# A decoder trunk on one core: the opening loop rebuilt (c broadcast through the identity, squares in three partial sums, no GpSimd products, a fixed order per k-tile, a seventh output tile)

## The chip, the core and the metric

The kernel runs on one core of one Trainium2 chip. The metric is the device time of one execution in microseconds (us); lower is better. The engines are TensorE (PE; its weight loads are PEld), VectorE (DVE), ScalarE (ACT), GpSimd (POOL) and SyncE (SP, which here only issues transfers). All numbers are float32. A product that has to keep float32 accuracy is made of "float32r" matmuls: each operand is split into a high part (h) and a remainder (l), and three matmuls h·h, l·h and h·l are added up in PSUM.

## The reference, cut to what matters

The sequence has 1024 tokens of width 1024, one layer. Around the change the reference computes this:

```python
c_act = jax.nn.silu(c)                          # c: (1, 1024)
mod = c_act @ ada_w[l] + ada_b[l]               # 6 x 1024 values
sh1, sc1, g1, sh2, sc2, g2 = jnp.split(mod, 6, axis=-1)
h = modulate(rmsnorm(x), sh1, sc1)              # h*(1+sc1)+sh1
u, q, k, v, r, z = jnp.split(h @ w_in[l], IN_SPLITS, axis=-1)
y_pool = pool_mixer(u, ...)                     # windows of 2, 4, 8, 16
y_gla = gla_mixer(q, k, v, r, z, ...)           # chunked gated linear attention
y = jnp.concatenate([y_pool, y_gla], axis=-1) @ w_out[l]
x = x + g1[:, None, :] * y
h = modulate(rmsnorm(x), sh2, sc2)
x = x + g2[:, None, :] * conv_ffn(h, ...)       # up, conv of width 3, silu, down
return rmsnorm(x) * final_norm
```

## The kernel before, in words

Everything is kept transposed: 128 channels on the partitions, tokens along the free dimension. The tokens are worked on as two halves of 512 (`hf` 0 and 1), the 1024 channels as eight k-tiles (`NK`). A matmul of 128x128 weights with 512 tokens is the unit of PE's work.

**The opening.** Eight tiles `x0[k]` of the first half are loaded. Line 230 (`sumsq_step`) squares each on ACT and line 234 adds the squares on DVE into one tile `nsa`; a float32 matmul with a matrix of ones (line 243, `ss`) sums over the partitions and spreads the sum, and ACT makes 1/rms of it with Ln and Exp (lines 245 and 246, `nr`). Meanwhile two float32 matmuls of `ones[0:1]` with the row `crow` spread c over all partitions, and ACT takes the silu of the PSUM tiles (line 558, `cb`). Six matmuls `warm` with no use stand at three places (`keep_warm`).

**The opening loop** goes over the eight k-tiles. For tile k it needs one column of sh1 and one of sc1. `mod_tile(t)` (line 214) makes one such column: it loads 128 rows of ada_w transposed (`ada`, 512 KB), multiplies with `cb` and sums along the row; a last small DVE instruction (line 225) adds the bias into `modv`. In its fast form product and sum are one DVE instruction (line 219). In its slow form POOL makes the product (line 222) and ACT the sum (line 223). The loop makes the shift columns k = 1 to 7 the slow way, and the shift of k = 0 and all scale columns the fast way. Then, for the tile: `mod_head` (line 267, DVE, `x`), the split of the weights `wh` (line 152, ACT) and `wl` (line 153, DVE), and `mod_split`: `hh` (line 274, ACT) and `hl` (line 275, DVE). PE then makes 3 matmuls for each of six output tiles (q, k, two of r) and 2 for the gate input z (`pz`), so 20 per k-tile. All seven results accumulate in PSUM over the eight k-tiles.

**After the loop** a list of jobs, each one output tile of a projection (24 matmuls of 512 tokens), fills PE: first r2 and r3 of the first half, then v, the four u, then the second half (`k0 z q0 k1 v0..v3 q1`, `r0..r3`, `u0..u3`), the output projection, and the MLP. Beside them runs the gated linear attention (GLA): two gate matmuls `gp`, then for each half and each of two channel tiles seven levels of scores `sc`, state products `sp`, outputs `op` and norms `on`. These are spawned as "sides" that come due at times of the planner's own clock, which adds up the matmuls' sizes; PE's order is written out by hand in this way (`manual_schedule` for PE), while the other engines' order is made by a scheduler. A job can hold PE's order back until a side has got to a point (`until`): job q0 and q1 of the second half do so until the first half's GLA outputs stand in the order.

Of the kernel before, what the change touches and what calls it, by code (L numbers as in the profile page):

```python
# [53 lines left out]
def trunk_kernel(ctx, tc, xT, cvec, adaT, vecs, w_start, w_z, w_qkru, w_v, w_g2, w_pool,  # L54
# [94 lines left out]
    def split_w(raw, shape=(P, NK, P)):  # L149
        wh = wp.tile(list(shape), F32R, tag="wh", name="wh")  # L150
        wl = wp.tile(list(shape), F32R, tag="wl", name="wl")
        act.copy(out=wh, in_=raw)  # L152
        dve.tensor_tensor(out=wl, in0=raw, in1=wh.bitcast(F32), op=ALU.subtract)  # L153
# [33 lines left out]
    crow = raw4("crow", (1, NK * P))  # L187
    nc.scalar.dma_start(out=crow, in_=cvec)
# [25 lines left out]
    def mod_tile(t, fast, where=None):  # L214
        a = raw4(name="ada", shape=(P, NK * P)) if where is None else tmp(where, shape=(P, NK * P))
        nc.sync.dma_start(out=a, in_=adaT[t])
        acc = const.tile([P, 1], F32, name="macc", tag="macc", bufs=4)
        if fast:
            dve.scalar_tensor_tensor(out=a, in0=a, scalar=1.0, in1=cb, op0=ALU.mult,  # L219
                                     op1=ALU.mult, accum_out=acc)  # L220
        else:
            pool_e.tensor_tensor(out=a, in0=a, in1=cb, op=ALU.mult)
            act.activation(out=a, in_=a, func=AF.Copy, accum_out=acc)
        one_plus = 8 <= t < 16 or 32 <= t < 40
        dve.scalar_tensor_tensor(out=modv[:, t:t + 1], in0=acc, scalar=1.0 if one_plus else 0.0,
# [11 lines left out]
    def rstd_of(acc, own=None):  # L237
# [7 lines left out]
        act.activation(out=r, in_=out, func=AF.Ln, bias=epsb, scale=1.0 / 1024)
        act.activation(out=r, in_=r, func=AF.Exp, scale=-0.5)
# [19 lines left out]
    def mod_head(x, t, r, sc_c, k):  # L266
        dve.scalar_tensor_tensor(out=t, in0=x, scalar=modv[:, sc_c + k:sc_c + k + 1], in1=r,
                                 op0=ALU.mult, op1=ALU.mult)
        return t

    def mod_split(t, sh_c, k):
        h, l = s2(F32R, name="hh"), s2(F32R, name="hl")
# [1 line left out]
        act.activation(out=h, in_=t, func=AF.Identity, bias=sh, scale=1.0)  # L274
        mark["split"] = dve.scalar_tensor_tensor(out=l, in0=t, scalar=sh, in1=h.bitcast(F32),  # L275
                                                 op0=ALU.add, op1=ALU.subtract)
# [276 lines left out]

    keep_warm(6)
    for n in range(2):
        cps = ptile()
        mm(cps, ones[0:1], crow[:, n * T:n * T + T], True, True)
        last = act.activation(out=cb[:, n * T:n * T + T], in_=cps, func=AF.Silu)
# [742 lines left out]
```

## Time and profile before

| what | value |
|---|---|
| median of 3 runs | 1050.42 us (1049.86 to 1051.85) |
| the profiled execution | 1047.94 us |
| its span, first to last instruction | 1046.2 us |
| mean granted PE clock | 0.989 |
| PE busy in the span | 1001.2 us (96%) |
| DVE busy | 854.6 us (82%) |
| ACT busy | 549.2 us (52%) |
| POOL busy | 190.5 us (18%) |

The profiled execution is 2.5 us shorter than the median of the runs, and 1.7 us longer than its span. PE's records are pipelined: matmuls of 512 tokens that follow each other start about 0.23 us apart, though each record is about 0.39 us long, so the distance between starts is what counts. A row of the timeline gives start, length, engine, line, operation, output<-input, shapes, count, and in brackets the idle time of the engine before it with what ended it. Several executions of a row can stand together with their count.

### The profile page before, as it was taken

To read this page: it belongs to the slowest core of one execution; us is meant where nothing else is said; L and a number is where in the kernel's file an instruction comes from. 1 tells how busy PE (TensorE), PEld (TensorE's weight loads), DVE (VectorE), ACT (ScalarE), POOL (GpSimd) and SP (SyncE) were. 2 spreads that over 40 slices of the span, in tenths; PEclk is the share of its full clock that TensorE was granted. 3 is DMA by queue.
4 is the path that set the end of the run, shared out by engine and by line. 5 is a ranking of instruction groups with operands and counts; after the bars stand their busy time and mean duration, and the time that the engine had idled before them with its cause. 6 is when DMAs were issued, how large, how long until landed. Compare 5 with 4: busy or idle time off the path is not lost.

```text
span 1046.2 us, 12684 instructions
## 1 busy us (share of the span) xinstructions
PE 1001.2 (96%) x4481; PEld 815.4 (78%) x4481; DVE 854.6 (82%) x1197; ACT 549.2 (52%) x888; POOL 190.5 (18%) x163
## 2 busy tenths in 40 slices
PE   7989999998999989999999999999999999999995
PEld 5768868886777768877888888888888788888874
DVE  7967899689988849999977788777776776988883
ACT  5465585442733547665555455555554544644442
POOL 3437203222141030011100101101001000200210
PEclk8999999999999999999999999999999999999998
DMA  8743232455487442233222222332334787223642
GB/s 315 258 151 111 81 110 83 149 174 182 149 280 262 155 167 81 86 137 129 105 99 91 105 102 107 131 111 101 111 111 151 272 283 240 101 81 111 201 141 81
DMA packets 60817, 154.21 MB, mean 147 GB/s; under 512 B 6641, under 2 KB 9809, under 8 KB 60754
## 3 DMA queue, kind: packets, MB, share of 16 engines
q1 hardware_dynamic: 54192, 134.00, 37.8%
q0 software_dynamic: 4928, 17.30, 4.3%
q10 hardware_dynamic: 1634, 2.10, 0.6%
q8 instruction: 35, 0.57, 0.2%
q14 instruction: 28, 0.23, 0.1%
HBM read 127.69 MB, written 25.69 MB: 147 GB/s over the span
## 4 chain that ended last, share of the span: by engine, by line
PE 62%; DVE 23%; DMA 5%; ACT 4%; issue 4%; POOL 2%; SPq 0%; POOLq 0%; ACTq 0%; DVEq 0%
PE dn L107 18%; PE upy L107 14%; PE upx L107 9%; PE upz L107 9%; PE pp L107 8%; DVE wl L153 3%; DVE ada L219 2%; DMA ada<-in_adaT_dram 2%; DVE xs L802 2%; DVE hl L275 2%; POOL le L347 1%; DVE la L376 1%; DVE ua L812 1%; DVE lq L359 1%; PE ss L107 1%
## 5 line engine op out<-in xcount | busy, mean ns | idle before, releaser
L107 PE MATMUL dn<-xs 128*128 128x512 f32 (+1 forms) x480 | 111.1, 386 | 1.7 <-DVE xs L802 1.3
L107 PE MATMUL dn<-ws 128*128 128x512 f32 x456 | 108.3, 394 | 2.3 <-DVE xs L1110 2.3
L107 PEld LDWEIGHTS dn<-xs 128*128 128x128 f32 x480 | 88.5, 188 | 21.1 <-DVE xs L802 2.1
L107 PEld LDWEIGHTS dn<-ws 128*128 128x128 f32 x456 | 86.7, 190 | 20.9 <-issue 2.7
L107 PE MATMUL upy<-sh,xs 128*128 128x512 f32 x264 | 86.6, 390 | 2.1 <-DVE cb L944 2.1
L107 PE MATMUL upy<-sh,ws 128*128 128x512 f32 x264 | 86.4, 389 | 0.0
L153 DVE TENSOR_TENSOR wl<-raw,wh 128x1024 fp32r<-128x1024 f32 (+1 forms) x50 | 64.2, 1285 | 27.1 <-ACT wh L152 26.8
L997 POOL DMA_DIRECT2D gd<-y x22 | 12.0, 546 | 375.7 <-DVE y L996 358.7
L107 PE MATMUL pp<-hh,wh 128*128 128x512 f32 x176 | 73.7, 419 | 2.7 <-ACT hh L274 1.4
L107 PE MATMUL pp<-hl,wh 128*128 128x512 f32 x176 | 70.8, 402 | 4.8 <-DVE hl L275 4.8
L107 PE MATMUL pp<-hh,wl 128*128 128x512 f32 x176 | 70.8, 402 | 2.6 <-DVE wl L153 2.6
L802 DVE TENSOR_TENSOR xs<-ua,xs 128x512 fp32r<-128x512 f32 x78 | 60.6, 782 | 14.8 <-ACT xs L801 14.8
L802 DVE TENSOR_TENSOR ws<-ua,ws 128x512 fp32r<-128x512 f32 x76 | 55.1, 727 | 15.7 <-ACT ws L801 15.7
L107 PE MATMUL upx<-hh,xs 128*128 128x512 f32 x192 | 62.8, 392 | 2.5 <-DVE x L693 2.5
L801 ACT CAST ws<-ua 128x512 fp32r<-128x512 f32 x76 | 47.0, 622 | 34.4 <-PE upy L107 17.2
L152 ACT CAST wh<-raw 128x1024 fp32r<-128x1024 f32 (+1 forms) x50 | 50.4, 1008 | 26.8 <-DMA raw<-in_w_out_dram 10.8
L801 ACT CAST xs<-ua 128x512 fp32r<-128x512 f32 x78 | 48.1, 622 | 30.5 <-PE upy L107 17.4
L812 DVE TENSOR_TENSOR ua<-ua 128x512 f32<-128x512 f32 x88 | 60.2, 687 | 2.1 <-DMA ua<-in_w_up_dram 0.3
L347 POOL TENSOR_TENSOR le<-b 128x512 f32<-128x512 f32 x24 | 37.1, 1549 | 134.1 <-DVE lq L359 53.8
L107 PE MATMUL upz<-sh,ws 128*128 128x512 f32 x184 | 60.4, 389 | 0.0
L937 DVE SCALAR_TENSOR_TENSOR y<-ca,vec,y 128x1023 f32<-128x1023 f32 (+1 forms) x44 | 56.3, 1280 | 4.3 <-ACT y L934 3.5
L107 PEld LDWEIGHTS upy<-sh,xs 128*128 128x128 f32 x264 | 49.5, 188 | 13.2 <-DVE cb L944 2.9
(261 smaller groups left out, 2521.2 us busy)
## 6 DMA issues: line engine op xcount, KB each, us to landing
ua<-in_w_up_dram SPq DMA_DIRECT2D x49, 512.0 KB, 3.4
ada<-in_adaT_dram SPq DMA_DIRECT2D x32, 512.0 KB, 3.4
gd<-y POOLq DMA_DIRECT2D x22, 512.0 KB, 2.9
raw<-in_w_qkru_dram SPq DMA_DIRECT2D x18, 512.0 KB, 3.3
da<-gd SPq DMA_DIRECT2D x36, 256.0 KB, 2.8
da<-in_w_down_dram SPq DMA_DIRECT2D x36, 256.0 KB, 3.4
raw<-in_w_out_dram SPq DMA_DIRECT2D x16, 512.0 KB, 4.4
x<-in_xT_dram SPq DMA_DIRECT2D x24, 256.0 KB, 4.3
```

What stands on the lines that cost most here:

```text
L107: pe.matmul(out=out, lhsT=lhsT, rhs=rhs, start=start, stop=stop, skip_group_check=more)
L152: act.copy(out=wh, in_=raw)
L153: dve.tensor_tensor(out=wl, in0=raw, in1=wh.bitcast(F32), op=ALU.subtract)
L219: dve.scalar_tensor_tensor(out=a, in0=a, scalar=1.0, in1=cb, op0=ALU.mult, op1=ALU.mult, accum_out=acc)
L275: mark["split"] = dve.scalar_tensor_tensor(out=l, in0=t, scalar=sh, in1=h.bitcast(F32), op0=ALU.add, op1=ALU.subtract)
L347: pool_e.tensor_tensor(out=e.rearrange("p (n h) -> p n h", n=nb), in0=b.rearrange("p (n h) -> p n h", n=nb), in1=bb[:, :, 0, h - 1:h].broa ...
L359: dve.tensor_tensor(out=ql.rearrange("p e (n h) -> p e n h", h=h), in0=q2.rearrange("p e (n two h) -> p e n two h", two=2, h=h)[:, :, :, 1 ...
L801: act.copy(out=h, in_=src)
L802: dve.tensor_tensor(out=l, in0=src, in1=h.bitcast(F32), op=ALU.subtract)
L812: eng.tensor_tensor(out=out, in0=a, in1=b, op=ALU.subtract)
L937: dve.scalar_tensor_tensor(out=y[:, sh:], in0=c[:, :S - sh], scalar=cw[j], in1=y[:, sh:], op0=ALU.mult, op1=ALU.add)
L997: nc.gpsimd.dma_start(out=gd[i], in_=ya)
```

## The change

The opening and its loop are written anew; the work after the loop keeps its code, but for the job r2, which the loop now does itself.

- c comes in as a 128x8 tile `cc`. Its silu is taken once on that small tile. Eight float32 matmuls, with one column of `cc` broadcast as the 128x128 stationary operand and the identity (`ident`, a part of `cft`) as the moving one, make the spread c; ACT copies the two PSUM tiles into `cb` after its last square.
- `cft` is loaded at the start, on ACT's queue, and no longer in the loop.
- The squares of x0..x3 are made on DVE, those of x4..x7 on ACT; they are added in three groups (4, 2, 2), and three matmuls `ss` add the groups in PSUM. The useless matmuls now number 8, 2 and 13.
- Both columns of each k-tile are made the fast way on DVE; the POOL products and the ACT sums of the loop are gone.
- The loads of tile k+2 are issued at tile k (`start_loads`), the ada tiles from five buffers in turn (`lo`, `lr`, `la`, `lb`, `lb`).
- `issue_after` fixes the order of a k-tile: on DVE two products, `mod_head`, `wl`, `hl`; on ACT `hh` of a tile, then `wh` of the next.
- Weights of a seventh output tile, r2, are in `w_start` (448 KB a tile in place of 384), and the loop makes it: 23 matmuls per k-tile in place of 20. Its PSUM tile is the single one of pool `m`. Job r2 is gone from the list after the loop, as `put_r(pq[6], 0, 2)` shows.

```diff
@@ split_w, mod_tile, rstd_of, mod_split
+    def later(inst):
+        return nullcontext() if inst is None else tc.issue_after(inst.ins)
-    def split_w(raw, shape=(P, NK, P)):
+    def split_w(raw, shape=(P, NK, P), act_after=None, dve_after=None):
...
-        act.copy(out=wh, in_=raw)
-        dve.tensor_tensor(out=wl, in0=raw, in1=wh.bitcast(F32), op=ALU.subtract)
+        with later(act_after):
+            act.copy(out=wh, in_=raw)
+        with later(dve_after):
+            mark["wl"] = dve.tensor_tensor(out=wl, in0=raw, in1=wh.bitcast(F32), op=ALU.subtract)
...
-        if fast:
+        with later(late):
             dve.scalar_tensor_tensor(out=a, in0=a, scalar=1.0, in1=cb, op0=ALU.mult,
                                      op1=ALU.mult, accum_out=acc)
-        else:
-            pool_e.tensor_tensor(out=a, in0=a, in1=cb, op=ALU.mult)
-            act.activation(out=a, in_=a, func=AF.Copy, accum_out=acc)
@@ opening
-    keep_warm(6)
-    for n in range(2):
-        cps = ptile()
-        mm(cps, ones[0:1], crow[:, n * T:n * T + T], True, True)
-        last = act.activation(out=cb[:, n * T:n * T + T], in_=cps, func=AF.Silu)
-    exp_ln(last)
-    keep_warm(6)
-    r0 = rstd_of(acc0)
-    keep_warm(6)
-    pq = [ptile() for _ in range(4)]
-    pq += [stile("pr"), stile("pr"), stile("pz")]
+    WARM = (8, 2, 0, 13)
+    def start_loads(k):
+        got = []
+        for t in (k, 8 + k):
+            a = tmp(("lo", "lr", "la", "lb", "lb")[ada_n[0] % 5], shape=(P, NK * P))
+            ada_n[0] += 1
+            nc.sync.dma_start(out=a, in_=adaT[t])
+            got.append(a)
+        raw = raw4(shape=(P, 7, P))
+        nc.sync.dma_start(out=raw, in_=w_start[k])
...
+    last = act.activation(out=cc, in_=cc, func=AF.Silu)
+    exp_ln(last)
+    loads = [start_loads(k) for k in range(2)]
...
+    for k in range(NK):
+        mm(cps[k // 4][:, k % 4 * P:k % 4 * P + P], cc[:, k:k + 1].broadcast_to([P, P]), ident,
+           True, True)
+    keep_warm(WARM[1])
+    ss = stile("ss")
+    parts = []
+    for k in range(NK):
+        sq = s2(name="sq")
+        if k < 4:
+            dve.tensor_tensor(out=sq, in0=x0[k], in1=x0[k], op=ALU.mult)
+        else:
+            last = act.activation(out=sq, in_=x0[k], func=AF.Square)
+        if k in (0, 4, 6):
+            parts.append(sq)
+        else:
+            added = dve.tensor_tensor(out=parts[-1], in0=parts[-1], in1=sq, op=ALU.add)
+        if k in (3, 5, 7):
+            mm(ss, ones, parts[-1], k == 3, k == 7)
...
+    with tc.issue_after(last.ins):
+        for n in range(2):
+            act.copy(out=cb[:, n * T:n * T + T], in_=cps[n])
+    r0 = rstd_from(ss)
+    keep_warm(WARM[3])
+    pq = [ptile() for _ in range(4)]
+    pq += [stile("pr"), stile("pr"), mtile("pr"), stile("pz")]
@@ the loop over k
-        mod_tile(k, k == 0, ("lo", "lr", "la")[k % 3])
-        with tc.issue_after(mark["split"].ins) if k else nullcontext():
-            mod_tile(8 + k, True, "lb")
-        wh, wl = load_w(w_start[k], (P, 6, P))
...
-        hs[0][k] = mod_split(mod_head(x0[k], x0[k], r0, 8, k), 0, k)
+        if k + 2 < NK:
+            loads.append(start_loads(k + 2))
+        after = mark["split"] if k else added
+        for t in (0, 1):
+            after = mod_tile(8 * t + k, loads[k][0][t], after)
+        with tc.issue_after(after.ins):
+            t = mod_head(x0[k], x0[k], r0, 8, k)
+        wh, wl = split_w(loads[k][1], (P, 7, P), mark["hh" if k else "exp"], mark["head"])
+        hs[0][k] = mod_split(t, 0, k, mark["wl"])
...
-        for n in range(6):
+        for n in range(7):
             mm3(pq[n], wh[:, n], wl[:, n], *hs[0][k], k == 0, k == NK - 1)
...
+    put_r(pq[6], 0, 2)
...
-    run_jobs([job_r(0, 2), job_r(0, 3)])
+    run_jobs([job_r(0, 3)])
...
-    a["w_start"] = np.concatenate([q, k, r[:, 0:2 * P]], axis=1).reshape(NK, P, 6, P)
+    a["w_start"] = np.concatenate([q, k, r[:, 0:3 * P]], axis=1).reshape(NK, P, 7, P)
```

Three places show how the instructions move. The first is DVE's order for the second k-tile of the loop, k = 1. Before (`lb` is the ada tile of the scale column, `macc` the sum that goes into `modv`; two sums arrive, one of them from ACT):

```order
L219 SCALAR_TENSOR_TENSOR lb_279,macc_281<-lb_279,cb_154 128x1024
L225 SCALAR_TENSOR_TENSOR modv_153<-macc_275,vec_136 128x1
L225 SCALAR_TENSOR_TENSOR modv_153<-macc_281,vec_136 128x1
L267 SCALAR_TENSOR_TENSOR x_121<-x_121,modv_153,nr_211 128x512
L153 TENSOR_TENSOR wl_287<-raw_284,wh_286 128x768
L275 SCALAR_TENSOR_TENSOR hl_292<-x_121,modv_153,hh_291 128x512
```

And the same tile of the change, where `la` holds the ada tile of the shift column:

```order
L226 SCALAR_TENSOR_TENSOR la_175,macc_306<-la_175,cb_155 128x1024
L232 SCALAR_TENSOR_TENSOR modv_154<-macc_306,vec_138 128x1
L226 SCALAR_TENSOR_TENSOR lb_177,macc_309<-lb_177,cb_155 128x1024
L232 SCALAR_TENSOR_TENSOR modv_154<-macc_309,vec_138 128x1
L277 SCALAR_TENSOR_TENSOR x_123<-x_123,modv_154,nr_229 128x512
L158 TENSOR_TENSOR wl_314<-raw_179,wh_313 128x896
L287 SCALAR_TENSOR_TENSOR hl_318<-x_123,modv_154,hh_317 128x512
```

DVE has one product of 1024 columns more in the tile, and `wl` grew from 768 to 896 columns. The second place is the opening of PE's order, of the change:

```order
L107 MATMUL pp<-ones 128x128 x8
L107 MATMUL pp<-cft,cc 128x128 x8
L107 MATMUL pp<-ones 128x128 x2
L107 MATMUL ss<-sq,ones 128x512 x3
L107 MATMUL pp<-ones 128x128 x13
```

Before it had `warm` x6, two 128x512 matmuls of `crow`, `warm` x6, one `ss` and `warm` x6. The third place is the end of the first half's GLA on PE, channel tile 1. Before, 18 matmuls of job v of the second half (`pp`) stand between the two groups of outputs `op`, and 6 more between the second group and the norm `on`; their first rows are

```order
L107 MATMUL op_1764<-lb_585,st1_156 128x256
L107 MATMUL op_1764<-la_1386,v_1010 128x128 x2
L107 MATMUL pp_1626<-wh_1719,hh_1241 128x512
L107 MATMUL pp_1626<-wh_1719,hl_1242 128x512
L107 MATMUL pp_1626<-wl_1720,hh_1241 128x512
```

and in the change the same place reads, up to the first matmuls of job q1,

```order
L107 MATMUL op_1791<-lb_615,st1_157 128x256
L107 MATMUL op_1791<-la_1420,v_987 128x128 x2
L107 MATMUL op_1807<-lb_615,st1_157 128x256
L107 MATMUL op_1807<-la_1420,v_989 128x128 x2
L107 MATMUL op_1807<-la_1420,v_991 128x128 x2
L107 MATMUL on_1816<-lr_1790,ones_148 128x512
L107 MATMUL on_1820<-lr_1790,ones_148 128x512
L107 MATMUL pp_1849<-hh_1110,wh_1746 128x512
```

The 24 matmuls that stood there have moved ahead, since every job comes one job earlier against the GLA: the two groups of outputs and the two norms now follow each other with nothing between.

More of the change, by code (lines that the diff above doesn't have):

```diff
@@ L186, in trunk_kernel @@
     act.preload_act_table_set("silu_and_others")
-    crow = raw4("crow", (1, NK * P))
-    nc.scalar.dma_start(out=crow, in_=cvec)
+    cc = const.tile([P, NK], F32, name="cc")
+    nc.scalar.dma_start(out=cc, in_=ccol)
+    cft = ga.tile([P, NC_F], F32, name="cft")
+    nc.scalar.dma_start(out=cft, in_=cf)
     x0 = [s2(name="x") for _ in range(NK)]
@@ L212, in trunk_kernel, with mod_tile, mod_store @@
     cb = ga.tile([P, NK * P], F32, name="cb")
[L214 to L217, printed above, removed]
-        if fast:
+    def mod_tile(t, a=None, late=None):
+        if a is None:
+            a = raw4(name="ada", shape=(P, NK * P))
+            nc.sync.dma_start(out=a, in_=adaT[t])
+        acc = const.tile([P, 1], F32, name="macc", tag="macc", bufs=3)
+        with later(late):
             dve.scalar_tensor_tensor(out=a, in0=a, scalar=1.0, in1=cb, op0=ALU.mult,
                                      op1=ALU.mult, accum_out=acc)
-        else:
-            pool_e.tensor_tensor(out=a, in0=a, in1=cb, op=ALU.mult)
-            act.activation(out=a, in_=a, func=AF.Copy, accum_out=acc)
+        return mod_store(t, acc)
+    def mod_store(t, acc):
         one_plus = 8 <= t < 16 or 32 <= t < 40
-        dve.scalar_tensor_tensor(out=modv[:, t:t + 1], in0=acc, scalar=1.0 if one_plus else 0.0,
+        return dve.scalar_tensor_tensor(out=modv[:, t:t + 1], in0=acc, scalar=1.0 if one_plus else 0.0,
                                  in1=vec[:, V_ADAB + t:V_ADAB + t + 1], op0=ALU.add, op1=ALU.add)
@@ L578, in trunk_kernel, with keep_warm @@
                               op=ALU.subtract)
-        hs[0][k] = mod_split(mod_head(x0[k], x0[k], r0, 8, k), 0, k)
+        return got, raw
+    ada_n = [0]
+    last = act.activation(out=cc, in_=cc, func=AF.Silu)
+    exp_ln(last)
+    loads = [start_loads(k) for k in range(2)]
+    idle = ptile()
+    def keep_warm(n):
+        for _ in range(n):
+            mm(idle[:, 0:P], ones, ones, True, True)
+    keep_warm(WARM[0])
+    cps = [ptile() for _ in range(2)]
+    for k in range(NK):
+        mm(cps[k // 4][:, k % 4 * P:k % 4 * P + P], cc[:, k:k + 1].broadcast_to([P, P]), ident,
+           True, True)
@@ new lines, in trunk_kernel @@
+    with tc.issue_after(last.ins):
[5 more added lines that the diff above has]
+    pq += [stile("pr"), stile("pr"), mtile("pr"), stile("pz")]
+    for k in range(NK):
+        if k + 2 < NK:
[7 more added lines that the diff above has]
+        hs[0][k] = mod_split(t, 0, k, mark["wl"])
```

53 lines of the change are left out of this document (26 added, 27 removed).

## The prediction

> **What bounds the kernel now.** I read first the page, then the timeline of each engine over the opening, then the busy time by stretch and the chain of waits behind it.
>
> ```profile
> core 0: us, PE busy (x) PEld busy (x) DVE busy (x) ACT busy (x) POOL busy (x), PEclk, DMA share, GB/s
> 20.00:40.00 20.00, 18.39 (x67) 14.08 (x68) 19.86 (x28) 7.81 (x12) 8.63 (x4) 0.83 0.68 241
> 40.00:60.00 20.00, 18.40 (x80) 13.87 (x79) 18.90 (x27) 10.55 (x17) 8.17 (x6) 1.00 0.61 210
> 130.00:140.00 10.00, 7.89 (x33) 5.66 (x32) 10.00 (x18) 7.19 (x12) 0.02 (x1) 1.00 0.46 157
> ```
>
> PE is the bound of the whole (96% busy in the table above), but not of the opening loop: from 20 to 40 us DVE works 19.86 of 20 us, and PE runs at a mean clock of 0.83. Why DVE is full, the timeline shows:
>
> ```profile
> 14.18 2.36 POOL L222 TENSOR_TENSOR lr<-lr,cb 128x1024 f32<-128x1024 f32 x1 [12.01 <-ACT nr L246]
> 14.21 2.87 DVE L267 SCALAR_TENSOR_TENSOR x<-x,modv,nr 128x512 f32<-128x512 f32 x1 [0.94 <-ACT nr L246]
> 17.87 2.83 DVE L275 SCALAR_TENSOR_TENSOR hl<-x,modv,hh 128x512 fp32r<-128x512 f32 x1
> 25.06 0.95 DVE L153 TENSOR_TENSOR wl<-raw,wh 128x768 fp32r<-128x768 f32 x1
> 25.94 0.75 DVE L275 SCALAR_TENSOR_TENSOR hl<-x,modv,hh 128x512 fp32r<-128x512 f32 x1
> 26.61 1.22 DVE L219 SCALAR_TENSOR_TENSOR lb<-lb,cb 128x1024 f32<-128x1024 f32 x1
> 28.06 0.75 DVE L267 SCALAR_TENSOR_TENSOR x<-x,modv,nr 128x512 f32<-128x512 f32 x1
> 28.73 3.16 DVE L153 TENSOR_TENSOR wl<-raw,wh 128x768 fp32r<-128x768 f32 x1
> ```
>
> The same `x` takes 2.87 us beside a POOL product and 0.75 us without one, `hl` 2.83 against 0.75, `wl` 3.16 against 0.95. So every POOL product costs DVE about 2.1 us. PE shows what comes of it:
>
> ```profile
> 20.76 0.79 PE L107 MATMUL pp<-hl,wh 128*128 128x512 f32 x1 [2.37 <-DVE hl L275]
> 26.90 0.40 PE L107 MATMUL pr<-hh,wh 128*128 128x512 f32 x1
> 38.41 0.50 PE L107 MATMUL pp<-hl,wh 128*128 128x512 f32 x1 [0.85 <-DVE hl L275]
> 48.70 0.39 PE L107 MATMUL pp<-hh,wh 128*128 128x512 f32 x1
> 53.25 0.39 PE L107 MATMUL pp<-hh,wh 128*128 128x512 f32 x1
> 54.27 0.50 PE L107 MATMUL pp<-hl,wh 128*128 128x512 f32 x1 [0.64 <-DVE hl L275]
> 63.30 0.39 PE L107 MATMUL pp<-hh,wh 128*128 128x512 f32 x1
> ```
>
> PE works without a stop only from 20.76 us. A k-tile of 20 matmuls at full clock takes 48.70 to 53.25, so 4.55 us, 0.2275 us a matmul. The 14 matmuls from 20.76 to 26.90 take 6.14 us where 3.19 would do: 2.95 us lost to the half clock. Two waits for `hl` are shown (0.85 and 0.64 us idle, about 1 us each with the start-up); there is a third like them. At 63.30 the loop is over and the first job begins.
>
> **The opening, costed.** When is 1/rms ready, and when the first `hl`?
>
> ```profile
> L191 SPq DMA_DIRECT2D x<-in_xT_dram x8: 397/431/433, 0.8 to 4.0; - x8
> DMA to landing us min/median/max: 2.7/3.7/4.6
> 6.39 0.58 ACT L558 ACTIVATE cb<-pp 128x512 f32<-128x512 f32 x1
> 1.06 2.93 PE L107 MATMUL warm<-ones 128*128 128x128 f32 x12 [1.06 <-DVE oneb L210]
> 10.75 2.04 PE L107 MATMUL ss<-nsa,ones 128*128 128x512 f32 x2 [0.19 <-DVE nsa L234]
> 11.86 1.22 DVE L219 SCALAR_TENSOR_TENSOR lb<-lb,cb 128x1024 f32<-128x1024 f32 x1
> 13.12 0.16 DVE L225 SCALAR_TENSOR_TENSOR modv<-macc,vec 128x1 f32<-128x1 f32 x1
> 12.83 0.69 ACT L245 ACTIVATE nr<-ss,epsb 128x512 f32<-128x512 f32 x1 [1.86 <-PE ss L107]
> 13.55 0.63 ACT L246 ACTIVATE nr<-nr 128x512 f32<-128x512 f32 x1
> 25.18 0.72 ACT L274 ACTIVATE hh<-x,modv 128x512 fp32r<-128x512 f32 x1 [5.58 <-DVE x L267]
> ```
>
> The last tile of x is issued at 4.0 and lands at the latest 4.6 us later: 8.6. Its square on ACT (taken as long as Exp, 0.63) ends at 9.25, one DVE add (below 0.75) at 10.0. The seven adds of before no longer stand in a row behind ACT. The last `ss` costs 2.04 us at the half clock, about 1.0 at the full one: 11.0, Ln and Exp (0.69 + 0.63) 12.4. Meanwhile ACT copies `cb` twice after its last square (2 x 0.58): 10.45; then DVE makes two products with their `modv`, each between 1.26 us (11.86 to the start of `modv`) and 1.42 (to its end), taken as 1.35: 13.15. This is later than 12.4, so the products decide. Then `x` 0.75 and `hh` 0.72 follow, beside `wl` (0.95 x 7/6 = 1.1), and `hl` 0.75: 13.15 + 0.75 + 1.1 + 0.75 = 15.75. No POOL product lies beside them any more. PE works without a stop from about **15.8 in place of 20.76**.
>
> That holds if PE has got to the full clock. If not, its own queue decides: 18 useless or spreading matmuls of 0.49 us (2.93/6) from 1.06 reach 9.9, three `ss` of 2.04 reach 16.0, Ln and Exp 17.3, then `x`, `wl`, `hl` 19.9. Gain 0.9 us, and the 2.95 us of half clock come again. I take the full clock: PE is busy without a gap from 1.06, as it is from 20.76, where the full clock came 6.1 us later; so it should come by about 7.2.
>
> The Trainium skill, "TensorE: Matmul & The Clock Gate", section "Part 1: The HAM clock gate", puts the full clock after about 3.4 us of sustained matmuls, in a window that runs free, so after at most two windows, 6.8 us. By that rule `ss` at 10.75 should have been fast; the trace disagrees there (2.04 us), and agrees at 26.90. By the rule the opening goes as in my sum; by the row of `ss` as in the slow case.
>
> **The loop.** PE: 23 x 0.2275 = 5.23 us a tile. DVE: two products and their `modv` 2 x 1.35, `x` 28.06 to 28.73 0.67, `wl` 25.06 to 25.94 0.88 x 7/6 = 1.03, `hl` 25.94 to 26.61 0.67: together 5.07, all of it without POOL. So PE is the bound by 0.16 us a tile, with little to spare; a few single splits (`zw`, pool weights) use up the 1.3 us that this makes over eight tiles. Bounds: if DVE is slower by as much as a record exceeds a spacing, 0.08 x 5 instructions, a tile is 5.5 and the loop 2.2 us longer. Loads: two ada tiles and 448 KB of weights, 1.5 MB in 5.2 us, 290 GB/s. The loop before drew 210 to 241 GB/s, but it was held by buffers; in the opening `ada` landed as fast as they were issued. The loads two tiles ahead (10 us) cover a landing of 4.6. End: 15.8 + 8 x 5.23 - 0.2 = **57.4, against 63.30: 5.9 us gained**, though the loop does 24 matmuls more.
>
> **The job that is gone.** Those 24 matmuls, 5.46 us, leave the work after the loop. Whether PE gains them is decided where it would then run dry: at the end of the first half's GLA, where 24 matmuls stood among `op` and `on`.
>
> ```profile
> 192.06 0.61 PE L107 MATMUL op<-la,v 128*128 128x128 f32 x4
> 192.70 0.59 ACT L490 COPY lo<-op 128x512 f32<-128x512 f32 x1 [0.21 <-PE op L107]
> 193.32 0.63 ACT L491 ACTIVATE lr<-lo 128x512 f32<-128x512 f32 x1
> 196.62 0.59 PE L107 MATMUL op<-lb,st 128*128 128x256 f32 x2
> 198.29 0.48 PE L107 MATMUL pp<-wh,hh 128*128 128x512 f32 x1
> 199.77 1.88 PE L107 MATMUL on<-lr,ones 128*128 128x512 f32 x4
> 201.09 0.80 PE L107 MATMUL pp<-hh,wh 128*128 128x512 f32 x1
> ```
>
> On this time axis, the second group of `op` (196.62 to 198.29, 1.67 us) now begins at 192.4 and ends at 194.1. The first `on` waits for ACT's copy and square (to 193.95), the second for another 0.3 + 0.59 + 0.63 after 194.1, to 195.6; with its own 0.66 it ends at 196.3 where 201.09 stood. So 4.8 of 5.46 us stay.
>
> Against that stands the stretch around 130 to 140 us, in which DVE is 10.00 busy and PE 7.89. There DVE decides, and it is ahead only by the loop's 5.9 and one `wl` (L153, 1.23 to 1.3). On the other hand the order now puts a GLA level behind that point. If DVE holds PE there for good, the gain is 5.9 + 1.2 less one level of PE's GLA work that then comes later (about 1.6, `sc` and `sp`): 5.5 us. If not, 5.9 + 4.8 = 10.7. I take 9.0, a third of the way down, since part of DVE's work did move behind. From about 480 us on PE runs without waits in both, so what is won before stays won.
>
> Sum: 1047.94 - 9.0 = 1038.9 for the profiled execution, which lies 2.5 us under the median of the runs; for the median 1050.4 - 9.0 = **1041.4 us**.
>
> **Rivals.**
>
> (1) *The opening stays at the half clock* (19.9, above). Loop end 19.9 + 41.6 + 2.95 = 64.5, so 1.2 later than before; with 4.8 for the job the gain is 3.6: 1046.8. For it: `ss` at 2.04 us after nearly 10 us of PE work. Against it: those matmuls of `crow` used one partition, and there were gaps.
>
> (2) *DVE bounds the middle.* The 5.5 us above: 1044.9. For it: the row 130 to 140. Against it: from 140 on PE is the chain.
>
> (3) *Slower: DVE work moved ahead of the GLA.* Since jobs come one earlier, the second half's gates go before the last GLA levels of the first half.
>
> ```profile
> 69.88 0.70 DVE lq L322
> 70.95 1.04 DVE b L326 x3
> 76.69 1.05 PE L107 MATMUL dg<-hsel,le 128*128 128x2 f32 x8 [2.55 <-POOL le L390]
> 77.74 5.84 PE pp L107 x18
> ```
>
> A gate costs DVE 2 x 0.70 + 4 x 0.35 = 2.8 us, two 5.6, one more `wl` and one ada product 2.6: 8.2. If all of this holds up the GLA and PE has nothing in between, the job's gain is idle time, and an idle stretch of 2.55 us makes the next 18 matmuls take 5.84 in place of 18 x 0.2275 = 4.1. Balance 5.9 - 8.2 - 1.7 = -4.0: 1054.4. It decides once more than 5.9 us of DVE work is pulled ahead of the last level. Against it: the sum of DVE's work up to q1 doesn't grow.
>
> (4) *The change doesn't do what it says*: POOL's products were no cost, or the 0.16 us a tile is not there and the loop is bound by DVE and loads, so that loop and job cancel: within 2 us of 1050.
>
> **How the numbers follow.** The forecast 0.57, with a range of its own of 1037 to 1045; (1) 0.13; (2) 0.17; (3) 0.07; (4) 0.06. About 0.2% (2.1 us) is what can be told from no change. Faster are the forecast, (2) and most of (1): 0.85; the same most of (4) and a little of (1): 0.08; slower 0.07. The range goes from 1036 (nothing lost to DVE, and the opening 1 us earlier still) to 1049, which takes in (1) and (2).
>
> **What would show it.** Right: no POOL rows before the loop's end, `x` and `hl` at 0.75 us in every tile; the first `hl` matmul near 15.8; starts 0.23 us apart from there; the first job's matmul near 57.4; q1 beginning about 9 to 10 us before 201. Wrong: `ss` records of 2 us, loop starts 0.43 us apart, waits for `hl` or `raw` in the loop, or a PE idle stretch above 2.5 us before q1.

## The result, and the profile after

The change runs in **1043.69 us** (median of 7 runs, 1037.53 to 1047.21), the kernel before in 1050.42 (7 runs on the same chip, 1048.75 to 1056.59). The ratio is 0.9926, with a 95% interval of 0.9902 to 0.9949: about 7 us faster. The profiled execution of the change took 1043.22 us, with a span of 1041.2 and a mean granted clock of 0.986 (before 1047.94, 1046.2, 0.989), so these two traces differ by 5.0 us of span.

The page's row of busy time and the busy time by stretch (the second row names the columns) of the change:

```profile
PE 1002.2 (96%) x4507; PEld 819.5 (79%) x4507; DVE 848.8 (82%) x1212; ACT 541.9 (52%) x870; POOL 166.6 (16%) x156
core 0: us, PE busy (x) PEld busy (x) DVE busy (x) ACT busy (x) POOL busy (x), PEclk, DMA share, GB/s
20.00:40.00 20.00, 19.96 (x87) 15.35 (x87) 19.59 (x35) 7.01 (x9) 0.00 (x0) 1.00 0.91 336
```

From 20 to 40 us PE is now busy 19.96 of 20 us at the full clock (18.39 at 0.83 before), POOL does nothing (in the whole loop it has four memsets of 0.52 us and no product), and the loads draw 336 GB/s where 241 were drawn. DVE is still nearly full, 19.59. The opening on the timeline:

```profile
4.79 2.02 PE L107 MATMUL pp<-cft,cc 128*128 128x128 f32 x16 [0.21 <-DMA cft<-in_cf_dram]
9.31 2.84 PE L107 MATMUL ss<-sq,ones 128*128 128x512 f32 x6 [2.04 <-DVE sq L605]
11.13 1.23 DVE L226 SCALAR_TENSOR_TENSOR lo<-lo,cb 128x1024 f32<-128x1024 f32 x1 [1.11 <-DMA lo<-in_adaT_dram]
14.01 0.75 DVE L277 SCALAR_TENSOR_TENSOR x<-x,modv,nr 128x512 f32<-128x512 f32 x1
16.48 0.51 PE L107 MATMUL pp<-hl,wh 128*128 128x512 f32 x1 [0.42 <-DVE hl L287]
21.02 0.75 DVE L287 SCALAR_TENSOR_TENSOR hl<-x,modv,hh 128x512 fp32r<-128x512 f32 x1
26.14 0.75 DVE L287 SCALAR_TENSOR_TENSOR hl<-x,modv,hh 128x512 fp32r<-128x512 f32 x1
58.78 0.39 PE L107 MATMUL pp<-hh,wh 128*128 128x512 f32 x1
```

The first `hl` matmul starts at 16.48 in place of 20.76, a tile of DVE takes 5.12 us (21.02 to 26.14), and the first job's matmul starts at 58.78 in place of 63.30. So the loop ends 4.5 us sooner, with 24 matmuls more in it.

What becomes of these 4.5 us and of the job that is gone is seen by following the same pieces of work through both traces:

| start of | before, us | change, us | ahead by |
|---|---|---|---|
| first matmul after the loop | 63.30 | 58.78 | 4.5 |
| `dg` after PE's first long wait | 76.69 | 71.99 | 4.7 |
| first matmul of q1 | 201.09 | 201.07 | 0.0 |
| `dg` of the second half, channel tile 0 | 204.92 | 204.91 | 0.0 |
| `dg` of the second half, channel tile 1 | 280.31 | 277.77 | 2.5 |
| end of the span | 1046.2 | 1041.2 | 5.0 |

At 205 us the change has **nothing left**: the 4.5 us of the loop and the 5.5 us of the job are gone, 10.0 us within 140. PE's waits from 60 to 205 us in the change (what waited, for whom; us in total, times, longest):

```profile
PE gp L107 <- ACT le L322: 3.5, 2, 2.7
PE dg L107 <- POOL le L402: 2.6, 1, 2.6
PE pp L107 <- ACT k L312: 1.7, 1, 1.7
PE on L107 <- ACT lr L503: 1.6, 1, 1.6
PE pp L107 <- DVE wl L158: 1.3, 1, 1.3
```

These are 10.7 us; before they were 5.7 (dg 2.6, wl 2.1, gp 1.0). The three that are new or longer stand at the end of the first half, on the timeline of PE:

```profile
143.32 0.40 PE L107 MATMUL pp<-hl,zw 128*32 128x512 f32 x1
148.66 0.80 PE L107 MATMUL gp<-le,g2w 96*128 96x512 f32 x1 [2.66 <-ACT le L322]
168.77 0.51 PE L107 MATMUL pp<-wh,hh 128*128 128x512 f32 x1 [1.73 <-ACT k L312]
199.38 2.26 PE L107 MATMUL on<-lr,ones 128*128 128x512 f32 x4 [1.59 <-ACT lr L503]
```

The first row is the last matmul of job z, which makes the gate's input. The wait of 2.66 us is for the second half's gate, whose matmul stood at 159.07 before, and whose cast `le` on ACT comes late. ACT works there without idle time from a table load on; three of its ten rows up to that cast:

```profile
142.28 1.28 ACT L189 ACT_TABLE_LOAD   x1
146.62 0.56 ACT L312 COPY k<-pp 128x512 f32<-128x512 f32 x1
148.04 0.57 ACT L322 CAST le<-pp 32x512 fp32r<-32x512 f32 x1
```

The same place in the kernel before (last matmul of job z, cast, gate):

```profile
154.58 0.39 PE L107 MATMUL pp<-hl,zw 128*32 128x512 f32 x1
158.09 0.57 ACT L310 CAST le<-pp 32x512 fp32r<-32x512 f32 x1
159.07 0.48 PE L107 MATMUL gp<-le,g2w 96*128 96x512 f32 x1
```

From the end of job z to the end of the cast it took 3.7 us before (154.97 to 158.66) and 4.9 in the change (143.72 to 148.61), so ACT's late queue is 1.2 us of the wait. The larger part is missing filler: before, PE had 4.1 us of other matmuls between job z and the gate (12 `pp`, 3 `po`, 8 `sc`), in the change 2.3 us (6 `pp` and the 8 small `dg`).

And with idle PE comes the half clock. The same stretch of the two kernels, before first and then the change (columns as above; the clock is the number before the last two):

```profile
140.00:160.00 20.00, 20.00 (x100) 15.49 (x99) 19.84 (x36) 17.43 (x29) 1.15 (x1) 1.00 0.25 80
```

```profile
140.00:160.00 20.00, 17.34 (x73) 12.83 (x71) 16.97 (x29) 16.03 (x29) 4.22 (x3) 0.83 0.08 26
```

PE issued 73 matmuls there where it issued 100. Of the 10.0 us lost up to 205, 5.0 are additional idle time by the two lists of waits; the remaining 5.0 are what is left for the slower clock. The clock rows are of that size: 140 to 160 us as shown, 70 to 80 us (0.90 before, 0.66 in the change) and 80 to 90 us (0.93 and 1.00) give 20 x 0.17 + 10 x 0.24 - 10 x 0.07 = 5.1.

After 205 us the change wins again. PE's waits from 205 to 300 us, before and in the change:

```profile
PE pp L107 <- ACT us L515: 2.3, 1, 2.3
PE sp L107 <- DVE la L376: 2.0, 1, 2.0
PE pp L107 <- ACT wh L152: 1.3, 1, 1.3
PE op L107 <- DVE la L376: 0.8, 1, 0.8
PE pp L107 <- DVE wl L153: 0.5, 1, 0.5
```

```profile
PE pp L107 <- ACT us L527: 2.2, 1, 2.2
PE op L107 <- DVE la L388: 0.8, 1, 0.8
PE sp L107 <- DVE la L388: 0.4, 1, 0.4
```

6.9 us have become 3.4. What PE waited for here before, `sp`'s `la` above all, is now done when PE gets there; that DVE got ahead while PE stood still in the first half's last levels is a reading, not shown by a run. Up to 320 us the waits are 9.1 and 3.6 us, 5.5 less; against them stands the half clock that only the change has from 270 to 280 us (mean 0.83), 1.7 us. These 3.8 us are most of the 4.75 by which it leads at the last `sp` (315.56 for 320.31), and from there on the lead stays near 4.5 to 5.0.

### The profile page after: what moved, and what is told of

Its sections match the earlier page's. It is cut to its first block, busy times and chain, and to the rows that moved or that the text cites. A ratio compares the mean times of both kernels' runs of the same rounds, so it can differ in the third digit from the quotient of the medians.

```text
span 1041.2 us, 12710 instructions
## 1 busy us (share of the span) xinstructions
PE 1002.2 (96%) x4507; PEld 819.5 (79%) x4507; DVE 848.8 (82%) x1212; ACT 541.9 (52%) x870; POOL 166.6 (16%) x156
## 4 chain that ended last, share of the span: by engine, by line
PE 76%; DVE 12%; ACT 4%; DMA 4%; issue 2%; POOL 1%; SPq 0%; POOLq 0%; ACTq 0%; DVEq 0%
PE dn L107 18%; PE pp L107 16%; PE upy L107 15%; PE upx L107 11%; PE upz L107 10%; PE sc L107 2%; PE pr L107 2%; DVE ada L226 1%; DVE wl L158 1%; DVE xs L852 1%; PE ss L107 1%; DVE la L388 1%; DVE us L534 1%; POOL le L359 1%; DMA ua<-in_w_up_dram 1%
## 5 line engine op out<-in xcount | busy, mean ns | idle before, releaser
L852 DVE TENSOR_TENSOR xs<-ua,xs 128x512 fp32r<-128x512 f32 x78 | 60.7, 783 | 14.8 <-ACT xs L851 14.8
L156 ACT CAST wh<-raw 128x1024 fp32r<-128x1024 f32 (+1 forms) x49 | 50.4, 1029 | 39.5 <-PE pp L107 10.7
L107 PE MATMUL pp<-hh,wh 128*128 128x512 f32 x168 | 70.1, 417 | 0.5 <-ACT hh L285 0.5
L107 PE MATMUL pp<-hh,wl 128*128 128x512 f32 x168 | 66.7, 397 | 1.3 <-DVE wl L158 1.3
L107 PE MATMUL pp<-hl,wh 128*128 128x512 f32 x168 | 66.7, 397 | 0.5 <-DVE hl L287 0.4
L987 DVE SCALAR_TENSOR_TENSOR y<-cb,vec,y 128x1023 f32<-128x1023 f32 (+1 forms) x44 | 56.3, 1280 | 2.4 <-ACT y L984 2.1
```

The costliest lines, as they stand in the source:

```text
L107: pe.matmul(out=out, lhsT=lhsT, rhs=rhs, start=start, stop=stop, skip_group_check=more)
L852: dve.tensor_tensor(out=l, in0=src, in1=h.bitcast(F32), op=ALU.subtract)
L987: dve.scalar_tensor_tensor(out=y[:, sh:], in0=c[:, :S - sh], scalar=cw[j], in1=y[:, sh:], op0=ALU.mult, op1=ALU.add)
```

## The experiments

Three questions were asked: where the job's 5 us went, what the half clock costs and who causes it, and whether the POOL products were really the price of the loop. Each ratio is against the kernel before on the same chip, with its 95% interval. None of the kernels leaves out a part of the computation.

### The job back where it was

The loop with six tiles, `job_r(0, 2)` after it as before, all else as in the change:

```diff
-        for n in range(7):
+        for n in range(6):
...
-    run_jobs([job_r(0, 3)])
+    run_jobs([job_r(0, 2), job_r(0, 3)])
```

> The change, but with six output tiles in the loop and job r2 back behind it; the order of PE behind the loop is then that of before. Theory A (the new opening makes the gain; the job moved into the loop gives it back, since at the first half's end the gate matmuls and the missing filler make PE wait): loop bound by DVE at about 4.95 us a tile, loop end near 55.6 us in place of 63.3, and the 7.7 us stay up to the first half's end (second half's first dg near 197 in place of 204.9); time 1041 to 1043, no slower than the change's 1043.7. Theory B (opening and moved job each bring their part, 4.5 and 2 to 3 us): 1046 to 1048, slower than the change.

Measured: 1043.02 us (1040.79 to 1044.62), ratio 0.9914 [0.9899, 0.9930]. The change without the moved job is as fast as the change: **the seventh tile brings nothing by itself**. The loop did not get shorter either; the matmul behind it stands at 59.55 where it stood at 58.78, because PE now waits for `hh` (1.3 us) and seven times for `hl` (2.2 in all) in it:

```profile
48.16 0.51 PE L107 MATMUL pp<-hh,wh 128*128 128x512 f32 x1 [1.34 <-ACT hh L285]
59.55 0.39 PE L107 MATMUL pp<-hh,wh 128*128 128x512 f32 x1
```

So in the loop the 24 matmuls cost next to nothing: with six tiles (20 x 0.231 = 4.6 us of PE) the loop goes at DVE's 5.0 us (`hl` at 20.71 and 25.73), with seven PE has 23 x 0.231 = 5.3. About 1 us of the 59.55, by estimate, is this execution's own: behind the wait at 48.16 PE has the half clock from 50.24 to 53.65. The 5.5 us of these matmuls are lost later, before 205: here the second half's `dg` stands at 201.1, 3.8 us ahead of the change and of the kernel before, with the same matmuls done up to there. After it the lead shrinks, to 1.4 us over the change at the second `dg` (276.4) and to nothing at the end (span 1042.8).

### The two places of the loss, one at a time

The order of the second half's jobs stands in two short lists, so the places can be taken away without touching a wait. First a filler ahead of q1, to fill the norm's place:

```diff
-    for names, mods_each in (("k0 z q0 k1 v0 v1 v2 v3 q1", 0), ("r0 r1 r2 r3", 2),
+    for names, mods_each in (("k0 z q0 k1 v0 v1 v2 v3 r0", 0), ("q1 r1 r2 r3", 2),
```

> The change, with jobs r0 and q1 of the second half exchanged: r0 fills PE among the last op and on of the first half, as 24 matmuls did before; the gates stay early. Theory A: the wait of 1.6 us for the square before on is gone, dg of the second half 2 to 4 us before 205: 1040 to 1042. Theory B (the missing filler costs nothing): 1043 to 1045.

Measured: 1043.85 us (1042.84 to 1047.19), ratio 0.9934 [0.9917, 0.9950]. PE no longer waits at `on`, but the waits at the gate (1.91 us, at 148.74) and for `k` (1.84, at 167.9) stay, and the time is that of the change. What was taken away at `on` comes back behind 205 us, where PE now waits 3.6 us for `sp`'s `la` (0.4 in the change): from 60 to 300 us the waits are 14.4 us, in the change 14.1.

Then the gates (job z) two jobs later:

```diff
-    for names, mods_each in (("k0 z q0 k1 v0 v1 v2 v3 q1", 0), ("r0 r1 r2 r3", 2),
+    for names, mods_each in (("k0 q0 k1 z v0 v1 v2 v3 q1", 0), ("r0 r1 r2 r3", 2),
```

> The change, with job z (and with it the second half's gates) two jobs later, behind q0 and k1; no filler at the first half's end. Theory A: no wait of 2.7 us at gp and none of 1.7 us behind it, no half clock from 144 to 156 us: 3 to 5 us less than the change, 1039 to 1041. Theory B (the wait only moves to another place, since DVE and ACT have the same work before the first half's end): 1043 to 1045.

Measured: 1043.78 us (1042.78 to 1046.12), ratio 0.9929 [0.9914, 0.9943]. PE's waits at the second half's gates are gone, and the wait at the norm has grown from 1.59 to 4.16 us:

```profile
196.70 2.92 PE L107 MATMUL on<-lr,ones 128*128 128x512 f32 x3 [4.16 <-ACT lr L503]
```

From 60 to 300 us its waits are 14.8 us. Taking away one loss alone brought nothing, in either run: the wait that was removed came back at a later place.

### Both places at once

```diff
-    for names, mods_each in (("k0 z q0 k1 v0 v1 v2 v3 q1", 0), ("r0 r1 r2 r3", 2),
+    for names, mods_each in (("k0 r0 z q0 k1 v0 v1 v2 v3", 0), ("q1 r1 r2 r3", 2),
```

Job r0, which nothing in the GLA needs, comes ahead of the gates, and q1 goes to the next list.

> The change, with job order k0 r0 z q0 k1 v0..v3 and q1 behind them: gates as late as before the change, and the filler at the first half's end restored. Theory A: both losses gone, the loop's 4.5 us and the job's 5.5 us both stay: 1037 to 1040. Theory B: 1043 to 1045.

Measured: **1038.14 us** (5 runs, 1035.63 to 1039.25), ratio 0.9869 [0.9853, 0.9885]. It is the fastest kernel here, 5.5 us below the change by the medians and 6 by the ratios (the two ran on different chips). PE's waits from 60 to 220 us are now those of the kernel before, without one at the second half's gates or at the norm:

```profile
PE dg L107 <- POOL le L402: 2.5, 1, 2.5
PE pp L107 <- DVE wl L158: 1.9, 1, 1.9
PE gp L107 <- ACT le L322: 0.8, 1, 0.8
```

Its second half's `dg` stands at 203.82, with job r0's 24 matmuls done ahead of it: 1.1 us and 5.5 in front of the kernel before, in an execution whose opening was 2.3 us later than the change's (first `hl` matmul at 18.81, for 16.48). The waits from 220 to 300 us are 6.8 us again, so here the gain is the one made before 205; from 60 to 300 us they are 12.0 us, 2.1 less than in the change.

### The same lists in the kernel before

It might be that this order is better whatever stands in the loop. So the kernel before got the same two lists, and nothing else.

> The kernel before with the job lists of e4_both (job r0 between k0 and z, q1 in the next list) and nothing else; its opening and loop stay as they were. Theory A: the 5 us that e4_both lies below the change are the moved job's gain, which a late queue at the second half's gates ate in the change. The kernel before has no such loss (its waits of PE from 60 to 205 us are 5.7 us, and none is at the second half's gates or at the norm), so the lists bring it nothing: 1050 us, within 2 us, and PE's waits from 60 to 220 us stay near 5.7. Theory B: the order of the lists is worth about 5 us whatever the loop, and has nothing to do with the moved job: about 1045. Theory C: in the kernel before the filler taken from between the outputs op and the norms is missing there, so it gets slower by up to 2 us: about 1052, with waits at op or on.

Measured: 1053.64 us (10 runs, 1051.32 to 1057.47), ratio 1.0027 [1.0009, 1.0046], so 2.9 us **slower**. Theory B falls: the order is worth 5.5 us only together with the moved job. A said 1050 within 2 us, and is off by the rest; C has the direction (1052 was expected) but not the place. Up to 205 us PE waits 6.7 us, with 1.1 more for `k` and nothing new at `op` or `on`; after it the level `sp` of the second half waits 3.6 us for `la` where the kernel before had 2.0, but others have become shorter: from 60 to 600 us the waits are 21.4 us against 21.7. So its waits do not show what makes this kernel slower. The clock shows a part: in its profiled execution PE has the half clock from 136.94 to 140.35 us, behind a wait of 2.13 us for `wl`, and the kernel before keeps the full clock behind the same wait (2.11). That is 1.7 of the 3.2 us by which it is behind at the second half's `dg` (213.60 with job r0's 5.5 us done, for 204.92); the wait for `k` is another 1.1. Whether the other nine executions lost their time in the same way is not known; over all runs the mean granted clock is 0.986 for 0.987, about 1.4 us.

### The gap at the first `dg`

All kernels up to here wait about 2.5 us for POOL at the first `dg` (at 71.99 in the change) and in nearly all profiles the half clock follows. With both places mended, the pause in the first GLA generator was doubled, which puts 15 matmuls more ahead of `dg`:

```diff
-        yield 3.0
+        yield 6.0 if (hf, ct) == (0, 0) else 3.0
```

> As the version with both (r0 moved, gates late), and the first GLA pair's first pause raised from 3.0 to 6.0 units of the planner's clock, so that PE has 15 more matmuls between the second gate matmul and dg, where it sat idle for 2.55 us. Theory A (that idle time costs itself and half a window of the half clock behind it): 2 to 4 us less than 1038, so 1034 to 1036. Theory B (the GLA chain decides, and later DVE waits take the gain): 1037 to 1040.

Measured: 1054.43 us (12 runs), ratio 1.0042 [1.0022, 1.0062], 16 us slower by the medians than without this edit. What both theories expected failed. In the profile, which is of the slowest of the 12 runs (1060.10), `dg` did start without a wait, but PE's waits from 60 to 220 us are 14.9 us where they were 5.2, and most are new. The two largest:

```profile
PE op L107 <- DVE la L388: 3.9, 1, 3.9
PE pp L107 <- ACT k L312: 2.6, 1, 2.6
```

and in the stretch in which DVE is full, PE stands and goes at the half clock:

```profile
120.00:140.00 20.00, 14.08 (x56) 11.35 (x55) 19.16 (x36) 7.13 (x12) 1.06 (x3) 0.74 0.38 131
```

The pause moves the later levels of the GLA back by the 15 matmuls, and these are missing as filler behind it; that this is the cause is argued from the order, not tested further. The wait of 2.5 us was the cheaper place to stand.

### What the useless matmuls are for

The change with `WARM = (0, 0, 0, 0)`:

> The change without any of the useless matmuls (0, 0, 0, 0 in place of 8, 2, 0, 13). Theory A (they bring the full clock): spreading and sums at the half clock, 1/rms 1 to 2 us later, and the loop's first 3 to 6 us at the half clock, 1.7 to 3 us more: 1046 to 1049. Theory B (the spreading matmuls alone bring it, or the clock does not decide the opening): 1043 to 1045.

Measured: 1046.36 us (12 runs), ratio 0.9956 [0.9939, 0.9973], against 0.9926 with them: about 3 us, though the two intervals touch. The half clock is in the rows:

```profile
4.94 3.76 PE L107 MATMUL pp<-cft,cc 128*128 128x128 f32 x16 [4.94 <-DMA cft<-in_cf_dram]
10.08 4.28 PE L107 MATMUL ss<-sq,ones 128*128 128x512 f32 x6 [1.39 <-DVE sq L605]
```

The 16 spreading records take 3.76 us in place of 2.02, the six of `ss` 4.28 in place of 2.84, and the loop's first matmuls start 0.43 us apart until 23.3.

More of them were also tried, in the kernel with both places mended, since its profiled execution had waited 2.80 us ahead of `ss` and then spent 4.54 us in it:

```diff
-    WARM = (8, 2, 0, 13)
+    WARM = (8, 11, 0, 13)
```

> As e4, with 11 useless matmuls in place of 2 between the spreading matmuls and ss, which fill the idle 2.0 to 2.8 us there. Theory A (e4's profiled run lost 2.1 us in the opening since PE fell to the half clock in that gap, ss 4.54 us in place of 2.84): ss at 2.9 us, first hl matmul at 16.5 to 17.0, time 1036 to 1038 and a smaller spread. Theory B (the gap is too short to matter in most runs): 1038 to 1039, no different from e4.

Measured: 1039.68 us (5 runs), ratio 0.9902 [0.9886, 0.9919]. `ss` is short again in its profile (2.84 us, after 0.34 of idle PE), but the kernel is no faster than the one with 2 (1038.14). The slow `ss` was one execution's, not the rule: in the eight other profiles with 2 useless matmuls at this place the pause was 1.70 to 2.64 us and `ss` took 2.84. On the same chip ran the change once more, unaltered, to tie the two groups of runs together.

> The change itself once more, on the chip of e9 and e10, so that these are compared with it under the same conditions. Both theories: 1042 to 1045; above e4's 1038 by 4 to 7 us if e4's gain is one of the kernel and not of the chip.

Measured: 1043.05 us, ratio 0.9929 [0.9910, 0.9947], which repeats 0.9926.

### The POOL products alone, taken away and put back

The kernel before, with every column of the loop on DVE:

```diff
-        mod_tile(k, k == 0, ("lo", "lr", "la")[k % 3])
+        mod_tile(k, True, ("lo", "lr", "la")[k % 3])
```

> The kernel of before with one edit: all sixteen columns made the fast way on DVE, no POOL products. Theory A: no DVE row of 2.8 us or more in the loop, head of tile 0 at 14.2 in 0.75 us, first hl matmul near 16.5 in place of 20.8, then DVE bounds the loop at about 4.95 us a tile and some of its start is at the half clock; loop end 56 to 58 in place of 63.3: 1043 to 1046 against 1050 to 1051. Theory B (the seven more products of 1.35 us on a full DVE cost what the contention cost): 1049 to 1054.

Measured: 1046.72 us (12 runs, 1044.09 to 1049.90), ratio 0.9961 [0.9944, 0.9977], so 4.1 us from this line alone. The loop's last matmul of `pz` stands at 58.63 in place of 63.07, and the `x` that took 2.87 us takes 0.75. So this line alone is worth more than half of the change's 7 us. The other 3 us are a difference, not a measurement: of the rest only the useless matmuls were taken away singly.

The other way round: the change, with the shift columns of k = 1 to 7 multiplied on POOL and summed on ACT:

```diff
-        for t in (0, 1):
-            after = mod_tile(8 * t + k, loads[k][0][t], after)
...
+            pool_e.tensor_tensor(out=s, in0=s, in1=cb, op=ALU.mult)
+            act.activation(out=s, in_=s, func=AF.Copy, accum_out=acc)
+            after = mod_tile(8 + k, loads[k][0][1], after)
```

> The change, with the shift columns of k-tiles 1 to 7 made as before: product on POOL, sum on ACT. Theory A (a POOL product holds up the DVE instruction beside it by 2.1 us): DVE per tile 5.12 - 1.34 + 0.16 + 2.1 = 6.0 us against PE's 5.23, rows of 2.8 us for 512 columns on DVE return, loop end near 64.5 in place of 58.8: 1048 to 1050. Theory B (PE bounds the loop, DVE has room): no slower than the change, 1043 to 1045.

Measured: 1052.94 us (12 runs), ratio 1.0016 [1.0001, 1.0031]. The gain is gone, but this run is not a clean one. In ACT's queue the first sum, late behind POOL, stands ahead of the Exp that gives 1/rms:

```profile
17.88 1.06 ACT L628 ACTIVATE la<-la 128x1024 f32<-128x1024 f32 x1 [4.19 <-POOL la L627]
18.93 0.61 ACT L256 ACTIVATE nr<-nr 128x512 f32<-128x512 f32 x1
```

so `x` came at 19.58. The second version puts the sum behind the `hh` of the tile before:

```diff
-            act.activation(out=s, in_=s, func=AF.Copy, accum_out=acc)
+            with later(mark["hh"]):
+                act.activation(out=s, in_=s, func=AF.Copy, accum_out=acc)
```

> As e5, but ACT's sum of a tile is placed behind hh of the tile before, so that it no longer stands ahead of the Exp of 1/rms on ACT, where e5 lost 5 us. Theory A (contention alone costs little here: six hits of about 1.9 us, 11 us of DVE in the loop, against seven products of 1.34 us that DVE is rid of, 9.4 us): loop end 59 to 61 us, time 1044 to 1046. Theory B (what e5 lost was contention): 1050 to 1053.

Measured: 1054.54 us (12 runs), ratio 1.0040 [1.0028, 1.0052]. Theory A expected the loop to end at 59 to 61 us; its last matmul of `pz` stands at 70.32. Theory B has the cause right and its range a little low. Rows of POOL and of DVE:

```profile
15.24 2.35 POOL L627 TENSOR_TENSOR la<-la,cb 128x1024 f32<-128x1024 f32 x1 [13.08 <-DMA la<-in_adaT_dram]
22.62 2.42 POOL L627 TENSOR_TENSOR lr<-lr,cb 128x1024 f32<-128x1024 f32 x1 [1.18 <-DMA lr<-in_adaT_dram]
26.83 2.93 POOL L627 TENSOR_TENSOR lb<-lb,cb 128x1024 f32<-128x1024 f32 x1 [1.79 <-DMA lb<-in_adaT_dram]
```

```profile
15.36 3.19 DVE L158 TENSOR_TENSOR wl<-raw,wh 128x896 fp32r<-128x896 f32 x1
22.76 2.36 DVE L232 SCALAR_TENSOR_TENSOR modv<-macc,vec 128x1 f32<-128x1 f32 x2
27.42 3.42 DVE L226 SCALAR_TENSOR_TENSOR lo<-lo,cb 128x1024 f32<-128x1024 f32 x1
33.42 1.22 DVE L226 SCALAR_TENSOR_TENSOR la<-la,cb 128x1024 f32<-128x1024 f32 x1
```

Each of the seven POOL products stretches whatever DVE instruction meets it, by 2.07 to 2.20 us, and the length of what it meets makes no difference: `wl` takes 3.19 in place of 1.08, a product 3.42 in place of 1.22, and even a pair of single-column `modv` 2.36 in place of 0.23. (All of these read two tiles; an instruction that reads one was not met.) DVE saves a product of 1.35 us and pays 2.1 for it: from 27.42 to 33.42 a tile takes 6.0 us where it took 5.12. Over the loop that is 15.0 us paid for 9.4 saved. It is not all of the loss: the loop ends 11.8 us later than the change's, and DVE also stands 4.4 us for `wh` of ACT (1.17, 1.62, 1.62), which the order of this version brings.

## Why the prediction was right, and where it was not

The forecast was 1041.4 us, the measured median is 1043.69, inside both ranges. By its own steps the picture is more mixed: one term failed, a gain was left out, and the two cancel in part. That the number fell inside the ranges is partly luck.

- **The bound of the loop: right.** No POOL product before the loop's end, `x` and `hl` at 0.75 us in every tile, starts 0.23 us apart. The runs without and with POOL products confirm the cause from both sides (−4.1 us in the kernel before; the whole gain lost in the change, though there ACT's order has a part in it).
- **The opening: right in the mechanism, 0.7 us off.** First `hl` matmul at 16.48 for "15.8 in place of 20.76". The two products decide, as was argued; they came late because the ada tile `lo` landed late (1.11 us idle ahead of 11.13). The full clock came in time, so rival (1) did not happen.
- **The loop: a little too short.** 183 matmuls from 16.48 to 58.78 are 0.231 us each for the 0.2275 taken from one tile, 0.7 us in all. Together with the opening "5.9 us gained" measured 4.5.
- **The job: the step that failed.** "So 4.8 of 5.46 us stay" was worked out at one place, the two `op` and `on`, with the time axis up to there left as it was. There the wait is 1.59 us, where the sum left 0.66 for the loss. But the queue in front of it had changed as well. Each job now meets the GLA one job earlier, the second half's gate falls into ACT's fullest stretch (142 to 149 us), PE waits 2.66 us for it and 1.73 for `k`, and it slows to the half clock. q1 starts at 201.07 for "about 9 to 10 us before 201". This is the mechanism of rival (3), which got 0.07: gates of the second half ahead of the first half's last levels. It was given too little because the sum of DVE's work up to q1 doesn't grow; the gate came late by ACT's order (1.2 us), and above all PE had 1.8 us less filler ahead of it. The sign that was named for it, a PE idle stretch above 2.5 us before q1, is there (2.66), but it could not tell: the kernel before has one too, the 2.55 us at the first `dg`.
- **The allowance for DVE: not what happened.** It took 1.7 us off for the stretch 130 to 140, in case DVE held PE there. DVE holds PE for `wl` in both kernels, 2.11 us before (at 136.46) and 1.30 in the change (at 124.38), so nothing came off there. After 205 PE's waits fell by 3.5 us (6.9 to 3.4), and for that the prediction has no term.
- **"What is won before stays won"**: it was said of the time from 480 us on and held there (5.0 at the end), but between 63 and 205 us nothing stayed.

The sum was −9.0 us; the two profiled executions differ by −4.7, the medians by −6.7. The change's own runs spread by more than the difference of these two: from 1037.53 (clock 0.989) to 1047.21 (0.984), of which the clock explains about half, 0.005 x 1041 = 5.2 us. That the failed step was worth what was said of it is shown by the kernel with both places mended: 1038.14, 5.5 us less than the change, while the same lists without the moved job make the kernel before 2.9 us slower. That the 5.0 us beside the new waits are all half clock is worked out from the rows of stretches, not shown by a run of its own. Open is also the half of the spread that the clock does not explain.

## What to carry to other kernels

Work that is taken out of a static order is a gain only where the queue can use it: shifting all later work of one engine by one job moves every meeting with the other engines, so go through each producer that the shifted work waits for (here ACT's cast of the gate) and count the filler that is left ahead of it, not only at the place where the work stood. If two waits share one slack, mending one shows nothing; mend both before dropping the idea, and run the mend in the old kernel too, to see whether it belongs to the change. A POOL product beside DVE is not free help: here each cost DVE about 2.1 of its 2.35 us, whichever instruction it met.

## What the hardware showed that was not expected

- **A POOL product holds a DVE instruction up to its own end.** In the run with the sums ordered, POOL's product runs from 15.24 to 17.59, and DVE's `wl`, begun at 15.36, ends at 18.55: POOL's end plus 0.96 (without POOL this `wl` takes 1.08). The pair of `modv` ends at 25.12, POOL at 25.04. And it works the other way: the POOL product that starts at 26.83 takes 2.93 us in place of 2.35, with DVE's `hl` running to 27.50. The Trainium skill, "SBUF — State Buffer", section "SBUF: two separate sides", calls this an exclusive lock, taken for the whole instruction by whoever starts first; these rows agree, and they add that an instruction of a single column pays the full 2.1 us.
- **The half clock hangs on where a pause lies, not only on its length.** PE stood 2.80 us ahead of `ss` in the profile of the kernel with both places mended, and the same six records then took 4.54 us where 2.84 is the full clock's. Pauses of 2.04 us (the change), 2.59 and 2.64 us (the change with POOL products, ordered and not) at that place did not do it. The pause at the first `dg` is the same in both profiles of the change, and only in the first does the half clock follow, the eight records of `dg` taking 1.48 us in place of 1.05:

```profile
10.21 4.54 PE L107 MATMUL ss<-sq,ones 128*128 128x512 f32 x6 [2.80 <-DVE sq L605]
71.99 1.48 PE L107 MATMUL dg<-hsel,le 128*128 128x2 f32 x8 [2.58 <-POOL le L402]
72.16 1.05 PE L107 MATMUL dg<-hsel,le 128*128 128x2 f32 x8 [2.55 <-POOL le L402]
```

  In all the traces the half clock that follows a pause lasts 3.41 us or two or three times that (in the change 72.44 to 79.27 and 147.54 to 154.36), and its beginnings lie whole multiples of 3.41 us after the first full clock, which comes at another time in each execution (4.18 us in the change, 6.37 in its second profile). So one and the same pause costs the half clock in one execution and not in another; no run was made to test this apart. The Trainium skill, "TensorE: Matmul & The Clock Gate", section "Part 1: The HAM clock gate", has the clock fall after at least one idle window of about 3.4 us. Here 2.80 us sufficed, as did 2.58 at the first `dg`, so the measurement decides against that figure as the shortest pause.
- **Full clock at 3.9 to 6.4 us.** In the change the spreading matmuls run at full speed from 4.79, after 3.5 us of dense useless matmuls; in its second profile the same 16 records take 2.72 us in place of 2.02, and the first full clock is granted at 6.37. With both places mended it is granted at 3.91. The kernel before still had `ss` at the half clock at 10.75, and is granted the full clock at 16.64. (Ahead of the first full clock the traces have no clock record, and the clock column shows 1.00 there.) From the first matmul (1.06) these are 2.8 to 5.3 us with dense matmuls, which roughly agrees with the 3.4 us of sustained work that the same section states. Whether it was the one-partition matmuls or the short gaps that kept the kernel before slow was not tried apart.
